# Two transformer blocks on one core: block 2's second expert product turned, small expert blocks of block 1 with both halves side by side, and block 2's bias rows made in block 1

## The chip, the cores and the metric

The kernel runs on one core of a Trainium2 chip. The core has five engines with instruction streams of their own: PE (TensorE, matmuls; PEld is its weight load, which overlaps), DVE (VectorE), ACT (ScalarE), POOL (GpSimd) and SP (SyncE), which here only issues transfers. Sixteen DMA engines move data between DRAM and the on-chip memory; SP, ACT and POOL each issue transfers on a queue of their own. Each engine works through its instructions in the order in which they are written and waits by semaphores.

The metric is the device time of one launch in microseconds (us). Before the change three runs took 2931.6, 2932.4 and 2934.65 us, median 2932.4.

## The reference

512 tokens of 1024 features go through two blocks, all in fp32, cut here to what the change touches:

```
# block 1: retention + differential attention, then a two-level top-2 MoE
x = x + g1 * (merged @ w_out)
h2 = rmsnorm(x, norm_ffn) * (1 + sc2) + sh2
gp = softmax(h2 @ w_rg + b_rg); g_top, g = top_k(gp, 1)          # 4 groups
e_val, e = top_k((h2 @ w_re + b_re)[g], 2)                       # of 8 experts
for each chosen expert (32 in all, inner size 512):
    y = (silu(xb @ w1[e]) * (xb @ w3[e])) @ w2[e]
x = rmsnorm(x + g2 * sum(y * weight), norm_final)
# block 2: banded attention with a relative bias, pooling mixer, PEER
s = q k^T / 8 + rel_bias[t5_bucket(j - 128 - i)]                 # 8 heads, band of 192 keys
x = x + concat(attention, pool) @ w_out
h = rms_norm(x, norm2_g)
# PEER: 16384 experts of one row each, 8 heads, 16 chosen per head
act = gelu(h . u[expert]);  x = x + sum(gate * act * v[expert])
```

## The kernel before

**Numbers.** Every large fp32 product is made of three matmuls of half-width parts: a weight chunk `raw` (128 x 1024, 512 KB) is copied into a rounded part `hi` by ACT (L363) and the rest `lo = raw - hi` by DVE or now and then POOL (L365); the other operand is split in the same way. x.h, x.l and (rest of x).h add up in a PSUM bank of 128 x 512. There are eight banks, handed out and taken back by `B.get` and `B.put`.

**The stream of weights.** `Stream` (`W`) loads all chunks in the order of their use, on SP's queue (L352), each as soon as one of a few raw buffers is free, and splits them up to `W.ahead` chunks ahead.

**The order.** The instruction order of each engine is the order in which the Python code issues them. While a product runs, the code calls `tick()` after every few matmuls; each call advances the generators of `side` by one step (at most `side.most` of them live at once), or one step of the row work. So a generator's place in `side`, and the number of ticks, fix where its instructions stand between the others on every engine.

**Block 1's experts.** After the mixers, routing sorts the 1024 token-expert pairs into blocks of one expert each. The first two and the last three slots have 128 rows; slot z in between has min(128, 1024/(z+2)) rows rounded up to eights: 64 at z = 14 down to 40. Per block `gather` fetches rows on POOL, `turn` transposes and splits them, `gate_up` (L1479) makes both first products with the token rows as the stationary operand (r columns) and 512 columns of weights moving, `turn_a` transposes the result, `down` (L1537) makes the last product and `scatter` (L1522, write on POOL L1530) writes rows to DRAM. One expert of a small block takes 12 chunks and 72 matmuls of 512 columns.

**The end of block 1's mixers.** `go(MG, ev_x1, j)` is the product with w_out; per output row block a `rows_of` generator makes the squares (ACT L541), the products for norm and router (PE L526) and the transposes (PE L544) beside the running product.

**The start of block 2.** `combine` loads and adds the expert rows, `norms` makes the norm statistics (POOL and DVE L529, then DVE L536), and `band_bias` (L1765) makes the bias of the attention band: a product of bucket indicators with the bias table gives 8 rows of 511, POOL writes each 128 times to DRAM (`lb_d`, 2 MB, L1771) and loads it back with a skewed address (L1773).

**PEER.** The first 384 tokens are treated densely: `u_block` multiplies 128 experts' u rows with the tokens and takes gelu, 24 matmuls of 384 columns; `weigh` multiplies by the gates and splits; `v_group` (L2437) makes the second product for four blocks, with chunks of v as the stationary operand (128 experts x 128 features) and the 384 weighed token columns moving, 24 matmuls per block, output transposed (features x tokens). Each pair of v chunks ends in four DVE adds out of PSUM into the running sum `X4` (L529), eight adds per group. Half of the u blocks was computed in a stage before and waits in DRAM; in the last stage (the V stage, 32 groups) the groups alternate between held ones and ones whose u blocks are made just ahead. The last 128 tokens go by rows (`rows_out`, L2280): POOL gathers each expert row (L2291), DVE makes the dot and the weighted sum (L2308, L532), paced by ticks.

Of the kernel before, what the change touches and what calls it, by code (L numbers as in the profile page):

```python
# [22 lines left out]
P = 128  # L23
# [92 lines left out]
RG = 8  # L116


def block_rows(z):

    if z < NSTAT or z >= NE - NBIG:
        return P
    return min(P, -(-(2 * S // (z - NSTAT + NBIG + 1)) // RG) * RG)


def _konst():
# [28 lines left out]
    put("same32", e[:, None] == np.arange(NE)[None, :])  # L155
    dyn = e >= NSTAT
# [45 lines left out]
def _arrays(i):  # L202
# [28 lines left out]
    r["v"] = n["peer_v_2"][0].reshape(32, 2, 2, P, 2, 512).transpose(0, 4, 1, 3, 2, 5)  # L231
# [245 lines left out]
def build(tc, a, out, dump=None, stop=None):  # L477
# [171 lines left out]
    for i, g in enumerate(SEQ):  # L649
        if i + 1 < NG and SEQ[i + 1] >= AHEAD:  # L650
            add(U[4 * SEQ[i + 1]:4 * SEQ[i + 1] + 4])
        add([flat(a["v"][g, s, m]) for s in range(2) for m in range(2)])
# [81 lines left out]
    def body():  # L734
# [489 lines left out]

        xg = [get(2, True) for _ in range(3)]
# [3 lines left out]
        side.push(shift_rows())  # L1229
# [232 lines left out]

        def turn(z):
            hi, lo = [], []
            x = xg[blocks.index(z) % 3]
            r = block_rows(z)
            for s in range(2):
# [9 lines left out]
        act_t = {}  # L1477

        def gate_up(zs):  # L1479
            xs = [xts.pop(z) for z in zs]  # L1480
# [29 lines left out]
        def turn_a(z):  # L1510
            t = act_t.pop(z)
            ps = B.get()
            r = block_rows(z)
            for q in range(4):
# [7 lines left out]
        def scatter(o, z):  # L1522
            y = yo[len(sc_ins) % 3]
            r = block_rows(z)
            acp(y[:r, :512], o[0][:r], AF.Copy, scale=gtab[:r, z:z + 1])
            ts(y[:r, 512:], o[1][:r], gtab[:r, z:z + 1])
# [10 lines left out]
        def down(zs, direct=False):  # L1537
# [3 lines left out]
            for i in range(4):  # L1541
                j, wh, wl = W.get()
                for (hi, lo), ps in zip(xs, o):
# [8 lines left out]
            for x, ps, z in zip(xs, o, zs):  # L1552
                put(x)
# [8 lines left out]
        def add_back(o, z):  # L1562

            parts = []
            r = block_rows(z)
            for n in range(2):
# [48 lines left out]
        dve.tensor_copy(toke, src_i)  # L1615
        yo = []

        def gate_places():
# [29 lines left out]
            mm(tab[:, 256:256 + NSLOT], tabT, perm, True, True)  # L1648
            yield
# [106 lines left out]
        onb, relb, lrow, band = get(), get(), get(), get()  # L1756
        nc.scalar.dma_start(onb[:32, :511], a["buckets"])
        nc.scalar.dma_start(relb[:32, :8], a["relb"])
# [6 lines left out]
        def band_bias():  # L1765
            ps = B.get()
            mm(ps[:8, :511], relb[:32, :8], onb[:32, :511], True, True)
            pool.memset(lrow[:8, 511:512], 0.0)
            acp(lrow[:8, :511], ps[:8, :511])
            B.put(ps)  # L1770
            pool.dma_start(lb_d[:], lrow[:8, :].unsqueeze(1).to_broadcast([8, P, 512]))  # L1771
            lb = lb_d[:]
            pool.dma_start(bmv, bass.AP(tensor=lb.tensor, offset=lb.offset + 127,  # L1773
                                        ap=[[511, P], [P * 512, 8], [1, 256]]))
            yield
# [3 lines left out]
            put([onb, relb, lrow, band])  # L1779
# [629 lines left out]
        X4 = [get(3, tight=True).ap for _ in range(2)]  # L2409
# [27 lines left out]
        def v_group(ws, last):  # L2437
            for s in range(2):
                bs = [B.get() for _ in range(4)]
                for m in range(2):  # L2440
                    c = W.get()
                    for d in range(4):
                        ps = bs[d][:, :ND]
                        for b in range(2):
                            o = b * 512 + d * P
                            h, l = c[1][:, o:o + P], c[2][:, o:o + P]
                            xh, xl = (x[:, :ND] for x in ws[2 * m + b])
                            mm(ps, h, xh, m + b == 0, False)
                            mm(ps, h, xl, False, False)
                            mm(ps, l, xh, False, m + b == 2)  # L2450
                        tick()
                        if m:
                            o = X4[s][:, d * ND:(d + 1) * ND]
                            tt(dve, o, o, ps, OP.add)
                            B.put(bs[d])
                            if last:
                                oc = (4 * s + d) * ND
                                (nc.sync, nc.scalar)[d % 2].dma_start(out[:, oc:oc + ND], o)
                    W.done(c[0])
            for x in ws:  # L2460
                put(x)
# [20 lines left out]
        for i in range(-1, NG):  # L2482
            if i == 0:
                for n in range(2):
                    nc.sync.dma_start(X4[n], flat(x4_d[:, 4 * n:4 * n + 4]))
# [11 lines left out]
            if w_c is not None:  # L2497
                v_group(w_c, i == NG - 1)
# [61 lines left out]

# [17 lines left out]
```

## Time and profile before

| what | value |
|---|---|
| runs | 2931.6, 2932.4, 2934.65 us, median 2932.4 |
| profiled execution | 2930.98 us, span 2929.2 us, mean granted PE clock 0.962 |
| busy share of the span | PE 93%, PEld 80%, DVE 76%, ACT 43%, POOL 26% |
| chain that ended last | PE 49%, DVE 29%, DMA 7%, issue 7%, ACT 7% |
| chain by line, first entries | PE bank L522 44%, DVE lo L365 7%, DVE arena L529 6% |
| DRAM traffic | 625.27 MB read, 62.06 MB written, 235 GB/s |

A busy share is an average over stages, so it does not tell what bounds one of them; the windows by stage do. In the views of instructions a row stands for one or several neighbouring instructions of a line: start, length, engine, line, operation, out<-in, tile sizes and count, and in square brackets the engine's idle time before it and what ended that. A matmul's length contains its way through the array, so neighbouring matmuls overlap: the distance from start to start is the time that one costs.

### The profile page before, as it was taken

How to read it: one execution, taken by the hardware profiler on the slowest of the kernel's cores; microseconds unless marked ns; L12 is line 12 of the kernel's file. 1: busy time of each engine (PE TensorE's matmuls, PEld its weight loads, DVE VectorE, ACT ScalarE, POOL GpSimd, SP SyncE). 2: the span in 40 equal slices, each digit the busy share in tenths (PEclk: the TensorE clock that was granted, in tenths of full speed). 3: DMA queues.
4: the chain of work that ended last, by engine and by line, in shares of the span. 5: the costliest groups of instructions: out<-in, count | busy, mean ns of one | idle time of the engine just before them, and what ended most of it. 6: DMA issues, size and time to landing. Idle time of an engine off the chain costs nothing.

```text
span 2929.2 us, 40594 instructions
## 1 busy us (share of the span) xinstructions
PE 2726.5 (93%) x14351; PEld 2342.7 (80%) x14351; DVE 2238.9 (76%) x4096; ACT 1262.3 (43%) x1859; POOL 757.6 (26%) x669
## 2 busy tenths in 40 slices
PE   6999999988999999985799988999999999999999
PEld 5887888877877665544567888899899999999999
DVE  7554566548898878863558998999688888888887
ACT  3432344345676766751334233444333333333332
POOL 6110021111212111101424555222132332333231
PEclk8999999998999999996899999999999999999999
DMA  6546322347998989975223335888989989999895
GB/s 221 165 124 208 130 73 72 119 140 248 351 323 320 341 305 334 353 247 113 68 69 113 97 118 186 294 293 295 306 296 300 306 287 311 296 297 312 283 304 187
DMA packets 242211, 673.83 MB, mean 230 GB/s; under 512 B 26497, under 2 KB 94513, under 8 KB 238288
## 3 DMA queue, kind: packets, MB, share of 16 engines
q1 hardware_dynamic: 176224, 467.14, 47.3%
q0 software_dynamic: 48256, 156.44, 15.9%
q10 hardware_dynamic: 17520, 47.57, 4.5%
q8 instruction: 115, 1.88, 0.3%
q14 instruction: 96, 0.79, 0.1%
HBM read 625.27 MB, written 62.06 MB: 235 GB/s over the span
## 4 chain that ended last, share of the span: by engine, by line
PE 49%; DVE 29%; DMA 7%; issue 7%; ACT 7%; POOL 1%; ACTq 0%; DVEq 0%; POOLq 0%; SPq 0%
PE bank L522 44%; DVE lo L365 7%; DVE arena L529 6%; DVE arena L532 4%; ACT hi L363 4%; DVE arena L2308 3%; PE bank L526 3%; PE bank L544 2%; DVE arena L538 2%; DVE arena_r L529 2%; ACT arena_r L541 2%; DMA lb_d<-arena 2%; DMA raw<-in_w_in_dram 1%; DMA raw<-in_w_ret_o_dram 1%; ACT arena L541 1%
## 5 line engine op out<-in xcount | busy, mean ns | idle before, releaser
L522 PE MATMUL bank<-arena_r,hi 128*128 128x384 f32 (+1 forms) x5792 | 1618.5, 360 | 42.0 <-DVE arena L529 29.0
L522 PEld LDWEIGHTS bank<-arena_r,hi 128*128 128x128 f32 x5792 | 1066.6, 192 | 123.2 <-issue 39.0
L522 PE MATMUL bank<-arena_r,lo 128*128 128x384 f32 (+1 forms) x2896 | 1032.1, 356 | 22.3 <-POOL lo L365 15.9
L365 DVE TENSOR_TENSOR lo<-raw,hi 128x1024 fp32r<-128x1024 f32 x490 | 602.7, 1242 | 219.9 <-ACT hi L363 215.1
L522 PEld LDWEIGHTS bank<-arena_r,lo 128*128 128x128 f32 x2896 | 554.2, 191 | 65.0 <-POOL lo L365 18.5
L363 ACT ACTIVATE hi<-raw 128x1024 fp32r<-128x1024 f32 x513 | 523.5, 1051 | 176.7 <-DMA raw<-in_v_dram 56.4
L541 ACT ACTIVATE arena<-bank 128x512 f32<-128x512 f32 (+7 forms) x478 | 251.2, 535 | 569.6 <-PE bank L522 437.7
L522 PE MATMUL bank<-hi,arena_r 128*128 128x512 f32 (+10 forms) x1064 | 346.2, 396 | 7.5 <-DVEq L2548 6.2
L541 ACT ACTIVATE arena_r<-arena 128x384 fp32r<-128x384 f32 (+1 forms) x160 | 87.5, 547 | 495.1 <-DVE arena L529 447.9
L529 POOL TENSOR_TENSOR arena<-arena 128x512 f32<-128x512 f32 (+10 forms) x172 | 180.8, 1069 | 380.3 <-ACT arena L541 274.3
L2291 POOL DMA_INDIRECT arena<-in_ur_dram,idx_i x128 | 156.0, 1219 | 401.0 <-DVE arena L2308 393.4
L2291 POOL DMA_INDIRECT arena<-in_vr_dram,idx_i x128 | 157.2, 1228 | 362.6 <-DVE arena L532 337.5
L522 PE MATMUL bank<-arena_r 128*128 128x512 f32 (+12 forms) x956 | 232.9, 398 | 4.4 <-DVE arena_r L538 4.4
L522 PEld LDWEIGHTS bank<-hi,arena_r 128*128 128x128 f32 (+10 forms) x1064 | 161.5, 152 | 89.9 <-issue 7.9
L529 DVE TENSOR_TENSOR arena<-arena,bank 128x384 f32<-128x384 f32 (+6 forms) x314 | 167.9, 570 | 72.3 <-PE bank L522 72.1
L522 PE MATMUL bank<-lo,arena_r 128*128 128x512 f32 (+10 forms) x532 | 209.2, 393 | 1.3 <-DVE lo L365 1.3
L522 PEld LDWEIGHTS bank<-arena_r 128*128 128x128 f32 (+10 forms) x956 | 151.4, 162 | 70.9 <-issue 4.3
L1530 POOL DMA_INDIRECT y_d<-arena,dst_i x34 | 53.0, 1558 | 502.1 <-ACT hi L363 212.4
L529 DVE TENSOR_TENSOR arena_r<-arena,arena_r 128x384 fp32r<-128x384 f32 (+1 forms) x160 | 94.6, 591 | 103.4 <-ACT arena_r L541 103.3
L532 DVE SCALAR_TENSOR_TENSOR arena<-arena 128x1024 f32<-128x1024 f32 (+3 forms) x136 | 165.5, 1217 | 0.2
L2308 DVE SCALAR_TENSOR_TENSOR arena<-arena 128x1024 f32<-128x1024 f32 x128 | 156.0, 1219 | 0.0
L529 DVE TENSOR_TENSOR arena<-arena 128x384 f32<-128x384 f32 (+8 forms) x272 | 125.3, 481 | 23.6 <-DMA arena<-g_d 9.9
(171 smaller groups left out, 2827.1 us busy)
## 6 DMA issues: line engine op xcount, KB each, us to landing
raw<-in_u_dram SPq DMA_DIRECT2D x128, 512.0 KB
raw<-in_v_dram SPq DMA_DIRECT2D x128, 512.0 KB
raw<-in_w_down_dram SPq DMA_DIRECT2D x72, 512.0 KB
raw<-in_w_gate_dram SPq DMA_DIRECT2D x70, 512.0 KB
raw<-in_w_up_dram SPq DMA_DIRECT2D x68, 512.0 KB
arena<-in_w_up_dram SPq DMA_DIRECT2D x60, 512.0 KB
arena<-in_w_gate_dram SPq DMA_DIRECT2D x58, 512.0 KB
raw<-in_w_in_dram SPq DMA_DIRECT2D x57, 512.0 KB
```

What stands on the lines that cost most here:

```text
L363: self.nc.scalar.activation(h, r, AF.Copy)
L365: e.tensor_tensor(l, r, h.bitcast(F32), op=OP.subtract)
L522: pe.matmul(ps, l, r, start=start, stop=stop)
L526: pe.matmul(ps, l, r, start=start, stop=stop, skip_group_check=True)
L529: e.tensor_tensor(o, x, y, op=op)
L532: dve.scalar_tensor_tensor(o, x, s, y, op0=op0, op1=op1)
L538: (e or dve).tensor_scalar(o, x, s1, s2, op0=op0, op1=op1)
L541: act.activation(o, x, f, **kw)
L544: pe.transpose(ps, x, kk("ident")[:n, :n])
L1530: i = pool.indirect_dma_start(out=y_d[:], out_offset=IOA(ap=dst_i[:r, z:z + 1], axis=0), in_=y[:r], in_offset=None, bounds_check=2 * S - 1 ...
L2291: pool.indirect_dma_start(out=b, out_offset=None, in_=a[tab], in_offset=IOA(ap=idx_i[:, j:j + 1], axis=0))
L2308: dve.scalar_tensor_tensor(b, b, 1.0, h3, op0=OP.mult, op1=OP.mult, accum_out=s_[:, j:j + 1])
```

## The change

1. **V stage.** `v_group` becomes `v_block`: the weighed tokens are the stationary operand (three tiles of 128 tokens, hi and lo parts) and the v rows move, 512 columns at a time: 18 matmuls of 512 columns per block. The sums of all 32 groups stay in six PSUM banks (`acc`) until the end, so there are no adds by DVE; two banks are left for the u blocks. The residual goes in as 24 fp32 products with the identity at the first group (`residual_in`). Its load goes on ACT's queue at the start of the stage. At the end six banks are copied out, by ACT and DVE in turn, and written in six transfers. v lies in DRAM in plain rows.
2. **Paired small blocks.** Slots 14 to 28 get exactly 64 rows. hi and lo of the rows lie side by side in 128 stationary columns (`beside`); `mm_pair` makes one matmul of all 128 columns with the weights' hi part and one of the 64 hi columns with the lo part: 48 matmuls instead of 72 per expert. The two halves of the result stand in the two halves of the partitions; for the first products they are added by eight small matmuls with `fold` in `turn_a`, for the last one in `scatter` (ACT, then DVE, for each half of the columns).
3. **Bias rows.** The product and the write to `lb_d` become a generator `bias_rows`, pushed with `shift_rows` ahead of the last product of block 1's mixers; its two small loads and the write are issued by SP. At the start of block 2 ACT issues the load of the finished band; `band_bias` keeps the last addition.

```diff
+        def bias_rows():
+            lrow, relb = get(), sm(8)
+            nc.sync.dma_start(lrow[:32, :511], a["buckets"])
+            nc.sync.dma_start(relb[:32], a["relb"])
+            for _ in range(4):
+                yield
+            ps = B.get()
+            mm(ps[:8, :511], relb[:32], lrow[:32, :511], True, True)
+            yield
+            acp(lrow[:8, :511], ps[:8, :511])
+            B.put(ps)
+            pool.memset(lrow[:8, 511:512], 0.0)
+            yield
+            nc.sync.dma_start(lb_d[:], lrow[:8, :].unsqueeze(1).to_broadcast([8, P, 512]))
+            lrow.put()
...
-        side.push(shift_rows())
+        side.push(bias_rows(), shift_rows())
...
+        def beside(o, x, n):
+            v = o.rearrange("p (q k r) -> p q k r", k=2, r=HB)
+            x = x.rearrange("p (q r) -> p q r", r=HB)
+            acp(v[:, :, 0, :], x)
+            tt(dve, v[:, :, 1, :], x, v[:, :, 0, :].bitcast(F32), OP.subtract)
+
+        def mm_pair(ps, x, wh, wl, first, last):
+            mmx(ps, x, wh, first, last)
+            mmx(ps[:HB], x[:, :HB], wl, False, last)
...
+        def gate_up_pair(z):
...
+                        mm_pair(ps, x[:, i * P:(i + 1) * P], wh[:, c], wl[:, c], i == 0, i == KT - 1)
...
+                if k:
+                    dve.tensor_copy(y.ap, ps)
+                else:
+                    acp(y.ap, ps)
...
+            if paired(z):
+                for k, y in enumerate(t):
+                    for q in range(4):
+                        o = (4 * k + q) * r
+                        mm(ps[:, o:o + r], y[:, q * P:(q + 1) * P], kk("fold"), True, True)
+                    y.put()
+                y, o = get(), getr()
+                acp(y[:, :256], ps[:, :256], AF.Silu)
+                tt(dve, y[:, :256], y[:, :256], ps[:, 256:], OP.mult)
+                B.put(ps)
+                beside(o.ap, y[:, :256], 4)
...
+            if paired(z):
+                for n in range(2):
+                    c = y[:r, 512 * n:512 * n + 512]
+                    acp(c, o[n][HB:], AF.Copy, scale=gtab[HB:, z:z + 1])
+                    stt(c, o[n][:r], gtab[:r, z:z + 1], c, OP.mult, OP.add)
...
         def band_bias():
-            ps = B.get()
-            mm(ps[:8, :511], relb[:32, :8], onb[:32, :511], True, True)
-            pool.memset(lrow[:8, 511:512], 0.0)
-            acp(lrow[:8, :511], ps[:8, :511])
-            B.put(ps)
-            pool.dma_start(lb_d[:], lrow[:8, :].unsqueeze(1).to_broadcast([8, P, 512]))
...
-            pool.dma_start(bmv, bass.AP(tensor=lb.tensor, offset=lb.offset + 127,
-                                        ap=[[511, P], [P * 512, 8], [1, 256]]))
...
-        def v_group(ws, last):
...
-                            mm(ps, h, xh, m + b == 0, False)
-                            mm(ps, h, xl, False, False)
-                            mm(ps, l, xh, False, m + b == 2)
-                        tick()
-                        if m:
-                            o = X4[s][:, d * ND:(d + 1) * ND]
-                            tt(dve, o, o, ps, OP.add)
...
+        acc = [[B.get() for _ in range(2)] for _ in range(ND // P)]
+        def residual_in():
+            for t, bs in enumerate(acc):
+                for q in range(KT):
+                    x = xl[q // 4][:, q % 4 * ND + t * P:q % 4 * ND + t * P + P]
+                    mmx(bs[q // 4][:, q % 4 * P:q % 4 * P + P], x, kk("ident"), q % 4 == 0, False)
+                tick()
+            put(xl)
+        def v_block(x, last):
+            c = W.get()
+            for t in range(ND // P):
+                xh, xl_ = (z[:, t * P:(t + 1) * P] for z in x)
+                for n in range(2):
+                    h, l = (z[:, n * 512:n * 512 + 512] for z in c[1:])
+                    ps = acc[t][n]
+                    mmx(ps, xh, h, False, False)
+                    mmx(ps, xl_, h, False, False)
+                    mmx(ps, xh, l, False, last)
```

SP's order at the end of block 1's mixers before (out<-in; `raw_65` to `raw_68` are the four raw buffers, w_out the last product of the mixers, w_gate the first expert chunks):

```order
L352 DMA raw_67<-in_w_out_dram 128x1024
L352 DMA raw_68<-in_w_out_dram 128x1024
L352 DMA raw_65<-in_w_out_dram 128x1024
L352 DMA raw_66<-in_w_gate_dram 128x1024
L352 DMA raw_67<-in_w_gate_dram 128x1024
L352 DMA raw_68<-in_w_gate_dram 128x1024
L352 DMA raw_65<-in_w_gate_dram 128x1024
```

The same place on SP with the change (the stream's load is now L363):

```order
L363 DMA raw_67<-in_w_out_dram 128x1024
L363 DMA raw_68<-in_w_out_dram 128x1024
L1239 DMA arena<-in_buckets_dram 32x511
L1240 DMA small<-in_relb_dram 32x8
L363 DMA raw_65<-in_w_out_dram 128x1024
L1250 DMA lb_d<-arena 1024x1x512
L363 DMA raw_66<-in_w_gate_dram 128x1024
L363 DMA raw_67<-in_w_gate_dram 128x1024
L363 DMA raw_68<-in_w_gate_dram 128x1024
L363 DMA raw_65<-in_w_gate_dram 128x1024
```

Two small loads stand before the last w_out chunk, and the write of the bias rows stands between it and the first gate chunk.

POOL's order at the start of block 2 before (`y_d` holds the expert rows, `small` the norm's statistics):

```order
L1530 DMA y_d<-arena,dst_i 1024x1024
L1593 DMA arena<-y_d 128x2048 x4
L529 TENSOR_TENSOR arena<-arena 128x1024 x3
L1768 MEMSET arena 8x1
L1771 DMA lb_d<-arena 1024x1x512
L1773 DMA arena<-lb_d 128x8x256
L529 TENSOR_TENSOR small<-small,kc 128x8 x6
```

The same place on POOL with the change (the adds are now L540):

```order
L1627 DMA y_d<-arena,dst_i 1024x1024
L1703 DMA arena<-y_d 128x2048 x4
L540 TENSOR_TENSOR arena<-arena 128x1024 x3
L540 TENSOR_TENSOR small<-small,kc 128x8 x6
L1949 COPY arena<-arena 128x1
```

The norm's small operations follow the adds of the expert rows directly.

DVE's order in the middle of the V stage before (L365 splits, L2308 and L532 the row work, L529 with a bank the adds out of PSUM):

```order
L365 TENSOR_TENSOR lo_76<-raw_67,hi_70 128x1024
L529 TENSOR_TENSOR arena<-arena,bank_89 128x384
L2308 SCALAR_TENSOR_TENSOR arena<-arena 128x1024
L529 TENSOR_TENSOR arena<-arena 128x16
L529 TENSOR_TENSOR arena<-arena,bank_90 128x384
L529 TENSOR_TENSOR arena<-arena,bank_88 128x384
L529 TENSOR_TENSOR arena<-arena,bank_87 128x384
L365 TENSOR_TENSOR lo_77<-raw_68,hi_71 128x1024
L532 SCALAR_TENSOR_TENSOR arena<-arena 128x1024
```

The same place on DVE with the change (L376 splits, L2412 and L543 the row work):

```order
L376 TENSOR_TENSOR lo_76<-raw_67,hi_70 128x1024
L2412 SCALAR_TENSOR_TENSOR arena<-arena 128x1024
L376 TENSOR_TENSOR lo_77<-raw_68,hi_71 128x1024
L543 SCALAR_TENSOR_TENSOR arena<-arena 128x1024
L2412 SCALAR_TENSOR_TENSOR arena<-arena 128x1024
L376 TENSOR_TENSOR lo_78<-raw_65,hi_72 128x1024
```

The adds out of the banks are gone; splits and row work alternate.

## Rows read from the trace of the kernel before

**Rows 1.** Windows: from:to, length, PE PEld DVE ACT POOL busy, clock, DMA share, GB/s.
```profile
1183.26:1236.95 53.69, 53.69 (x253) 27.30 (x254) 47.92 (x52) 40.18 (x52) 8.11 (x9) 1.00 0.95 353
...
1265.00:1330.00 65.00, 50.53 (x205) 26.86 (x204) 46.64 (x65) 29.50 (x35) 11.66 (x11) 0.86 0.83 292
...
2400.00:2640.00 240.00, 233.38 (x1331) 231.62 (x1329) 207.08 (x295) 79.78 (x113) 73.43 (x62) 0.99 0.91 299
```

**Rows 2.** The chain that ended last, start of block 2: start, us, what.
```profile
1343.33 45.93 DMA lb_d<-arena
...
1390.51 1.71 POOL small L529
...
1392.23 0.17 DVE small L529
```

**Rows 3.** Timeline of PE, start of block 2.
```profile
1393.36 3.67 PE L522 MATMUL bank<-arena,kc 128*128 128x512 f32 x4 [27.00 <-DVE arena L536]
```

**Rows 4.** The window right after that wait.
```profile
1393.36:1397.10 3.74, 3.74 (x5) 1.70 (x6) 0.73 (x4) 0.62 (x2) 0.00 (x0) 0.54 0.46 168
```

**Rows 5.** Timeline of DVE, start of block 2.
```profile
1361.40 0.17 DVE L538 TENSOR_SCALAR small<-small 128x4 f32<-128x4 f32 x1
```

**Rows 6.** DMA queues from 1348 to 1362: packets, MB, share (q0 POOL, q1 SP).
```profile
q0 software_dynamic: 174, 0.69, 47.6%
q1 hardware_dynamic: 72, 0.26, 6.8%
```

**Rows 7.** Timeline of SP, end of block 1's mixers.
```profile
562.52 27.36 SPq L352 DMA_DIRECT2D raw<-in_w_out_dram  x6
599.88 7.97 SPq L352 DMA_DIRECT2D raw<-in_w_gate_dram  x4
```

**Rows 8.** Timeline of ACT, end of block 1's mixers.
```profile
611.49 2.94 ACT L363 ACTIVATE arena_r<-raw 128x1024 fp32r<-128x1024 f32 x3
```

**Rows 9.** Timeline of PE, end of block 1's mixers.
```profile
615.81 0.61 PE L522 MATMUL bank<-arena_r,hi 128*128 128x512 f32 x2
...
616.49 0.61 PE L522 MATMUL bank<-arena_r,hi 128*128 128x512 f32 x2
...
617.17 0.95 PE L526 MATMUL bank<-kc,arena 128*128 128x1 f32 x8
```

**Rows 10.** Timeline of PE, small experts of block 1.
```profile
1192.04 5.72 PE L522 MATMUL bank<-arena_r 128*40 128x512 f32 x24
...
1260.14 0.39 PE L522 MATMUL bank<-hi,arena_r 128*40 128x512 f32 x1
1260.45 0.44 PE L544 MATMUL bank<-kc,arena 40*128 40x40 f32 x4
```

**Rows 11.** Timeline of DVE, small experts of block 1.
```profile
1193.01 4.62 DVE L365 TENSOR_TENSOR lo<-arena,hi 128x1024 fp32r<-128x1024 f32 x4
...
1200.64 0.68 DVE L529 TENSOR_TENSOR arena<-arena,bank 40x512 f32<-40x512 f32 x1 [0.74 <-PE bank L522]
```

**Rows 12.** Timeline of PE in the V stage.
```profile
2400.05 0.51 PE L522 MATMUL bank<-arena_r,hi 128*128 128x384 f32 x2
...
2400.57 0.51 PE L522 MATMUL bank<-arena_r,hi 128*128 128x384 f32 x2
```

**Rows 13.** Groups by line and shape from 2280 to 2640: count, busy us, mean ns.
```profile
L522 PE MATMUL bank<-arena_r,hi 128*128 128x384 f32 x1316 | 338.1, 338 | 11.4 <-DVE arena L529 11.3
...
L529 DVE TENSOR_TENSOR arena<-arena,bank 128x384 f32<-128x384 f32 x107 | 53.9, 547 | 0.0
```

**Rows 14.** Waits from 2280 to 2860: us in total, times, longest us.
```profile
PEld bank L522 <- issue: 27.0, 12, 3.9
PE bank L522 <- DVE arena L529: 23.5, 10, 3.6
```

**Rows 15.** Timeline of ACT, gelus of a group late in the V stage.
```profile
2868.71 0.47 ACT L541 ACTIVATE arena<-bank 128x384 f32<-128x384 f32 x1
...
2873.14 0.47 ACT L541 ACTIVATE arena<-bank 128x384 f32<-128x384 f32 x1
```

More of the change, by code (lines that the diff above doesn't have):

```diff
@@ L116 @@
 RG = 8
+HB = P // 2
 def block_rows(z):
@@ L1466, in turn @@
             r = block_rows(z)
+            if paired(z):
+                ps = B.get()
+                for q in range(KT):
+                    tr(ps[:, q * r:(q + 1) * r], x[:r, q * P:(q + 1) * P], r)
+                t = getr(2)
+                beside(t.ap, ps, KT)
+                B.put(ps)
+                xts[z] = t
+                return
             for s in range(2):
@@ L1477, in body @@
         act_t = {}
+        def gate_up_pair(z):
+            x = xts.pop(z)
+            t = []
+            for k in range(2):
+                ps = B.get()
+                for q in range(4):
+                    j, wh, wl = W.get()
+                    for s in range(2):
+                        i = 2 * q + s
+                        c = slice(512 * s, 512 * s + 512)
+                        mm_pair(ps, x[:, i * P:(i + 1) * P], wh[:, c], wl[:, c], i == 0, i == KT - 1)
+                    W.done(j)
+                    tick()
+                y = get()
+                if k:
+                    dve.tensor_copy(y.ap, ps)
+                else:
+                    acp(y.ap, ps)
+                B.put(ps)
+                t.append(y)
+            x.put()
+            act_t[z] = t
         def gate_up(zs):
+            if paired(zs[0]):
+                return gate_up_pair(zs[0])
             xs = [xts.pop(z) for z in zs]
@@ L1565, in add_back @@
             r = block_rows(z)
+            pair = z < NE and paired(z)
+            if pair:
+                r = P
             for n in range(2):
@@ new lines, in body @@
+        acc = [[B.get() for _ in range(2)] for _ in range(ND // P)]
+        def residual_in():
+            for t, bs in enumerate(acc):
+                for q in range(KT):
+                    x = xl[q // 4][:, q % 4 * ND + t * P:q % 4 * ND + t * P + P]
+                    mmx(bs[q // 4][:, q % 4 * P:q % 4 * P + P], x, kk("ident"), q % 4 == 0, False)
+                tick()
+            put(xl)
[3 more added lines that the diff above has]
+                xh, xl_ = (z[:, t * P:(t + 1) * P] for z in x)
+                for n in range(2):
+                    h, l = (z[:, n * 512:n * 512 + 512] for z in c[1:])
[3 more added lines that the diff above has]
+                    mmx(ps, xh, l, False, last)
+                    if last:
+                        y = get()
+                        if n:
+                            acp(y.ap, ps)
+                        else:
+                            dve.tensor_copy(y.ap, ps)
+                        oc = t * D + n * 512
+                        (nc.sync, nc.scalar)[n].dma_start(out[:, oc:oc + 512], y.ap)
+                    if not (n and t == 1):
+                        if (t, n) != (2, 1):
+                            tick()
+            W.done(c[0])
+            put(x)
@@ L2497, in body @@
             if w_c is not None:
-                v_group(w_c, i == NG - 1)
+                for b, x in enumerate(w_c):
+                    v_block(x, i == NG - 1 and b == 3)
     def overflow(src_i, add_back):
```

77 lines of the change are left out of this document (41 added, 36 removed).

## The prediction

> **What bounds the kernel now.** I read the windows by stage first, then the chain of waits in the one long hole, then the timelines around the three places that the change touches. In the windows the reader is to see that TensorE (PE) is close to full wherever the change works: all of 53.69 us over three small experts of block 1, and 233.38 of 240 us in the V stage, the last 850 us [rows 1]. So a matmul saved counts there only as far as VectorE (DVE) or the transfers do not take its place: DVE is busy 47.92 of the 53.69 us, and the transfers have a share of 0.95 in that window and 0.91 in the V stage [rows 1]. The chain shows the hole: the 2 MB write of bias rows to DRAM is issued at 1343.33 and takes 45.93 us, and a small POOL operation of the norm at 1390.51, which only queues behind the bias rows on POOL, ends last before PE goes on [rows 2]. PE waits 27.00 us for it [rows 3], and runs at a granted clock of 0.54, the lower of its two levels, for the 3.74 us after it [rows 4].
>
> **Part 1, the wait at the start of block 2 goes.** Without the bias write and the load on POOL's queue, the norm's POOL step follows its DVE operation of 1361.40 directly [rows 5]: 1361.57 + 1.70 on POOL, then 0.17 on DVE, and from there the 1.13 us between the chain's DVE row and PE's start (1393.36 - 1392.23): 1364.6. PE is busy with its products until 1366.4 (1393.36 - 27.00), so nothing is left of the wait. Gone: 27.00, and half of the 3.74 us at the lower clock, 1.9; less whatever the POOL step meets by then, 1. T1 = -28 (bounds -20, if the chain behind it has another late member, to -29). The load of the finished band goes on ScalarE's (ACT) queue at the start of block 2, issued earlier than now (the write that it follows is long done), so it cannot be later: 0.
>
> **Part 2, the same write moved to the end of block 1's mixers.** It is not gone: buckets, bias table and the write now stand in SP's queue, the queue of all weight loads, ahead of the first expert's gate chunks. The last mixer load is issued at 562.52 + 27.36 = 589.9, so the write can go out at about 591, once its row is made by then; the gate loads now go out from 599.88 [rows 7]. How long the write holds its transfer engines: 45.93 us in the chain; the lower bound is its packets, 0.476 x 16 x 14 us / 174 = 0.613 us each [rows 6], of which each of 8 source rows has 64: 39 us. While it ran in block 2, a 512 KB weight load issued on the other queue had moved only 0.26 MB after 14 us [rows 6]: half of it sat behind the write. The first gate chunk sits behind the same write, on the same queue. It lands, then, not soon after 600 but at 630 to 637.
>
> The Trainium skill ("DMA: Bandwidth & Descriptors", section "Queues, rings and completion order") says that on each transfer engine the descriptors of one queue's ring are consumed in ring order; the half load of [rows 6] fits that, though it was on another queue. By the rule the gate chunk cannot overtake the write; if it could, that would be the first rival below.
>
> Who waits: ACT's order puts three splits of the gate chunks (2.94 us) at 611.49, ahead of the operations that make the router's rows for the next row block [rows 8]; PE's product with these rows stands at 617.17 [rows 9], and PE's own products behind it cannot pass. So PE stops at about 617 and goes on when the chunks have landed, three splits and a square are through (3.5 us): 633.7 to 641, a stall of 17 to 24; I take 22, nearer the measured 45.93 than the packets' sum. Beside it 1.9 for the lower clock after the stall as in [rows 4], and the moved bias product, at most 3.67/4 = 0.9 [rows 3], in this stretch with PE full 0.5. T2 = +24 (bounds: +0.5, if the loads do not wait, to +30, if the write goes out later because its row is late on ACT). If the stall is hidden, what hides it would be PE work of the mixers ordered before the row products, and the order gives none.
>
> **Part 3, fifteen small experts with both halves side by side.** PE per expert: 72 matmuls of 512 columns become 48. 24 take 5.72 with the last one's tail, so 0.2317 from start to start [rows 10]: 16.7 become 11.1, with transposes and eight folds about 13.5 against 53.69/3 = 17.9 now. DVE does not shrink: four splits take 4.62 [rows 11], twelve 13.9, and the rest of its 47.92/3 = 16.0 is small operations. The change adds on it the copy of one product, the second halves of two splits and a second pass in the scatter: six operations of 256 to 512 columns for five small ones, by the 0.68 of one on 512 [rows 11] 5 x 0.68 = 3.4 in place of 2.1: 17.3. So the period goes to DVE's 17.3 plus handoffs, against 17.9: 0.3 to 0.6 less. Twelve chunks of 512 KB per expert, 6.29 MB, at 353/0.95 = 372 GB/s for a full share are 16.9 [rows 1], so transfers allow little more. Twelve of the fifteen lie where PE is full; the last three end in the window 1265 to 1330, where PE has 50.53 of 65 us, behind loads: 0 there. T3 = 12 x -0.35 = -4. Bounds: -9 (period 17.2, and 1 us at the end) to +13 (a DVE gap of 1 us per expert, since a full DVE hides no wait for ACT).
>
> **Part 4, the V stage.** Three matmuls of 384 columns take 2400.57 - 2400.05 = 0.52 [rows 12], so 0.1733 each; three of 512 columns, with the same full stationary operand, 616.49 - 615.81 = 0.68 [rows 9], 0.2267 each. V has 3072 of the first (532.4) and would have 2304 of the second (522.3): -10 in all. More lies in waits. In 360 us stand 1316 matmuls with a hi part, two of every three, so 1974 [rows 13]; two groups (four u blocks and eight V blocks) hold 288, so a period of 52.5, of which 288 x 0.1733 = 49.9 is matmul. The waits are for DVE's adds out of PSUM (23.5 us, 10 times) and issue behind them (27.0, 12 times) over 580 us [rows 14]. These adds go: 107 of 0.547 in the 360 us [rows 13], 16 per period, 7.7 to 8.8 us. DVE's busy 207.08 of 240 [rows 1], 45.3 per period, falls to 37, with the ACT handoffs in `weigh` about 42. So DVE is late no longer; next are the transfers: share 0.91 x 52.5 / 49.3 = 0.97, above the 0.95 of the experts' window. PE per period: 96 x 0.1733 + 144 x 0.2267 = 49.3; with a little lost to transfers 50.1, 2.4 less than now. Over 15.5 periods -37. Added: 24 fp32 products of 128 columns for the residual, priced by a fp32 product of 512 at the lower clock, 0.92 [rows 3], a quarter 0.23, half of that at the full clock: 2.8 to 5.5, I take 4. The load of the residual moves from SP to ACT's queue at the start of the stage, ahead of the first group of u blocks, which hides it: 0 (uncovered, 1.5 MB at the 299 GB/s of [rows 1], 5 us). At the end six evacuations replace eight adds and the last transfers are fewer and larger: 0 to +1. T4 = -33 (bounds -48, no waits left, to 0, below).
>
> **Sum.** -28 + 24 - 4 - 33 = -41 on the profiled 2930.98 us (1.8 of it outside the span of 2929.2): 2890. The median shown is 1.4 above that execution, so 2892.
>
> **The rivals.**
> 1. The gate loads do not wait behind the write (its packets run faster beside idle engines, or its row is ready much earlier). For: the transfers have under half their capacity used there, and 591 is only my reading of when the row is made. Against: [rows 6]. T2 = +1: 2869. Chance 0.20.
> 2. The V stage gives its gain back. Six of eight banks hold sums, so the u blocks have two: the next u block can start only when ACT has taken a bank, and its gelus stand 4.43 apart where they follow each other [rows 15], against 24 x 0.1733 = 4.16 of PE. A coupling of 2 us per group of u blocks, 16 groups, is 32; the transfers at 0.97 could cost as much. For: ACT's order mixes these gelus with splits that wait for loads. Against: 4.43 includes DVE waits that go. T4 = 0: 2925; chance 0.12, half of it within 2927 to 2938.
> 3. Slower. In a pair the stationary operand alternates between 128 and 64 columns with every matmul. If PE does not run on through such a switch, each matmul shows its full length, 0.39 to 0.40, in place of 0.2317 [rows 10]: 48 x 0.163 = 7.8 on 13.5, 21.3 per expert against 17.9; times 12 = +41 for T3: 2937. It decides as soon as a switch costs more than (17.9 - 13.5)/48 = 0.09. Against: the one switch in the trace, from a 512-column matmul at 1260.14 to 40-row transposes at 1260.45, lies 0.31 apart, 0.08 above the spacing [rows 10], which DVE's 17.3 would still cover. Chance 0.08.
>
> The Trainium skill ("TensorEngine Tiling (Array Packing)", section "Key Properties") says that a change of tiling mode drains TensorE, which is the third rival's mechanism if 64 columns count as another mode; the 0.31 of [rows 10] speaks against a full drain here.
>
> **Chances.** The forecast 0.60, the rivals 0.20, 0.12, 0.08. Below 2926.5 is faster by over 0.2% (about what a measurement of this kernel can tell from no change), to 2938.3 the same: faster 0.60 + 0.20 + 0.06 = 0.86, same 0.06 + 0.02, slower 0.06. The likeliest case with T2's and T4's bounds, 2872 to 2912; for 8 in 10 it reaches down into the first rival and up toward the second: 2864 to 2920.
>
> **What would show it.** T1: POOL's norm step right after 1361, no PE hole there. T2: a PE hole of 17 to 24 us right after the router rows' product near 617, with the write in the transfers and ACT's gate splits waiting for their load; without it the first rival. T3: DVE near 100% and PE under 85% in the window of the small experts, 17.2 to 17.6 each; the third rival shows 0.39 between starts with PE full. T4: no waits for DVE in the V stage, transfers near 0.97, a period near 50. The forecast is wrong if the stall or the V gain is off by more than 20 us.

## The result and the profile after

The changed kernel takes 2868.58 us (median of 4 runs, 2864.65 to 2872.04), the kernel before on the same chip 2933.53: a ratio of 0.9777, 95% interval 0.976 to 0.9795. Forecast were 2892, range 2864 to 2920. The direction and all four signs came out; the gain is 65 us where 41 were forecast, and how much of that was luck is said below.

Where it went is read from landmarks, the start of the same instruction in both profiled executions (span 2929.2 before, 2864.4 after), and the step from one landmark to the next is what a stage gained or lost:

| landmark | before | after | difference | step | forecast |
|---|---|---|---|---|---|
| last weight split by ACT before the bias rows | 560.2 | 556.4 | -3.8 | -3.8 | none |
| first store of the router's rows by ACT (mixers done) | 652.3 | 674.1 | +21.9 | +25.7 | T2 +24 |
| POOL's load of the expert rows (block 1 done) | 1314.1 | 1326.5 | +12.4 | -9.5 | T3 -4 |
| first load of gates for the V stage | 2077.6 | 2054.7 | -22.9 | -35.3 | T1 -28 |
| end | 2929.2 | 2864.4 | -64.8 | -41.9 | T4 -33 |

The first step lies ahead of every changed instruction. In a kernel that changes nothing before block 2 (the turned second product alone, below) this landmark lies at 556.8, so it is no part of the change.

**The stall in the mixers is there.** SP's timeline after: the bias write goes out at 586.79, one gate load behind it.

```profile
585.75 0.35 SPq L363 DMA_DIRECT2D raw<-in_w_out_dram  x1
586.79 0.85 SPq L1250 DMA_DIRECT2D lb_d<-arena  x1
595.06 7.53 SPq L363 DMA_DIRECT2D raw<-in_w_gate_dram  x1
```

ACT's and PE's timelines after: ACT's split of that load, which started at 611.49 before [rows 8], waits 23.23 us for it, and the product with the router's rows, at 617.17 before without a wait [rows 9], waits 21.64 us for ACT.

```profile
632.18 1.06 ACT L374 ACTIVATE arena_r<-raw 128x1024 fp32r<-128x1024 f32 x1 [23.23 <-DMA raw<-in_w_gate_dram]
...
636.32 1.87 PE L537 MATMUL bank<-kc,arena 128*128 128x1 f32 x8 [21.64 <-ACT arena L552]
```

**The wait at block 2's start is gone, and the slow stretch ahead of it is shorter.** POOL's timeline after: the norm's step follows 25.25 us behind the adds, with nothing between.

```profile
1341.58 2.35 POOL L540 TENSOR_TENSOR arena<-arena 128x1024 f32<-128x1024 f32 x1 [0.22 <-DMA arena<-y_d]
1369.18 2.61 POOL L540 TENSOR_TENSOR small<-small,kc 128x8 f32<-128x8 f32 x1 [25.25 <-DVE small L549]
```

The windows from the first product of block 2 to where the clock rises, before and after (length, PE and the other engines busy, granted clock, share, GB/s), show what the prediction did not count: in both PE is busy throughout, at the lower clock level in most of it, but before for 21.5 us and after for 7.7.

```profile
1335.90:1357.40 21.50, 21.45 (x74) 16.59 (x74) 7.75 (x10) 11.76 (x19) 1.14 (x1) 0.54 0.49 84
```

```profile
1350.90:1358.60 7.70, 7.64 (x28) 5.64 (x28) 6.53 (x9) 7.70 (x14) 0.00 (x0) 0.60 0.72 193
```

**The experts.** Two windows after: the first holds the one large two-block step among the small experts with its neighbours, the second six small experts in a row; then the same stretches before.

```profile
1074.50:1130.40 55.90, 55.90 (x281) 44.66 (x280) 48.67 (x53) 39.71 (x52) 15.27 (x10) 1.00 0.87 317
1136.60:1244.50 107.90, 95.70 (x446) 64.93 (x446) 101.87 (x109) 86.49 (x110) 11.97 (x18) 0.92 0.94 352
```

```profile
1052.30:1118.00 65.70, 65.70 (x313) 46.43 (x312) 47.77 (x52) 38.44 (x51) 8.54 (x8) 1.00 0.78 283
...
1123.70:1231.00 107.30, 107.30 (x505) 56.04 (x504) 96.22 (x104) 80.62 (x103) 16.28 (x18) 1.00 0.96 352
```

Six small experts take 107.9 us where they took 107.3: nothing is won there, PE has 12 us of idle time instead, and DVE is busy for 101.87. The window with the large step is 9.8 us shorter, about the whole of T3's step: there PE was the bound before (65.70 of 65.70, DVE 47.77) and still is.

Alternating the stationary operand costs no drain. PE's timeline after: 128 and 64 columns follow each other every 0.23 us, as the equal ones did [rows 10].

```profile
1104.10 0.39 PE L537 MATMUL bank<-hi,arena_r 128*128 128x512 f32 x1
1104.33 0.39 PE L537 MATMUL bank<-lo,arena_r 128*64 128x512 f32 x1
1104.56 0.40 PE L537 MATMUL bank<-hi,arena_r 128*128 128x512 f32 x1
```

**The V stage.** The window after that answers to the last of [rows 1]: PE is busy for all of it, and the list of PE's waits from 2250 to 2830 is empty, where it had the two of [rows 14].

```profile
2400.00:2640.00 240.00, 240.00 (x1172) 212.82 (x1171) 188.91 (x240) 88.49 (x121) 89.90 (x66) 1.00 0.93 318
```

1172 matmuls at 240 per two groups are 4.88 periods of 49.1 us. Without a count of matmuls, by the starts of DVE's splits in `weigh` (eight per two groups), fourteen periods take 690.8 us (2109.6 to 2800.4), 49.3 each, which is PE's own time by the prediction's prices; before they took 740.6 (2127.3 to 2867.9), 52.9 each. Forecast were 50.1 and 52.5.

### The profile page after: what moved, and what is told of

Read it like the earlier page. It is cut to its first block, busy times and chain, and to the rows that moved or that the text cites. A ratio compares the mean times of both kernels' runs of the same rounds, so it can differ in the third digit from the quotient of the medians.

```text
span 2864.4 us, 38446 instructions
## 1 busy us (share of the span) xinstructions
PE 2655.4 (93%) x13453; PEld 2239.4 (78%) x13453; DVE 2138.9 (75%) x3858; ACT 1285.0 (45%) x1876; POOL 796.8 (28%) x667
## 4 chain that ended last, share of the span: by engine, by line
PE 34%; DVE 15%; issue 2%; DMA 2%; ACT 1%; POOL 1%; ACTq 0%; another core or an unknown queue 0%; POOLq 0%; DVEq 0%
PE bank L537 19%; PE bank L533 15%; DVE arena L549 3%; DVE lo L376 2%; DVE arena L540 2%; DVE arena_r L540 1%; DVE arena L543 1%; DVE arena L2236 1%; DVE arena L2243 1%; DVE arena L2238 1%; DVE arena L2412 1%; DVE arena L2302 1%; ACT arena L552 1%; DMA arena<-g_d 1%; POOL arena L540 1%
## 5 line engine op out<-in xcount | busy, mean ns | idle before, releaser
L533 PE MATMUL bank<-arena_r,hi 128*128 128x384 f32 (+1 forms) x3744 | 1084.0, 370 | 16.7 <-ACT arena L552 7.5
L376 DVE TENSOR_TENSOR lo<-raw,hi 128x1024 fp32r<-128x1024 f32 x490 | 602.5, 1244 | 223.4 <-ACT hi L374 213.2
L533 PEld LDWEIGHTS bank<-arena_r,hi 128*128 128x128 f32 x3744 | 687.8, 191 | 92.9 <-issue 8.2
L533 PE MATMUL bank<-arena_r,lo 128*128 128x384 f32 (+1 forms) x1872 | 683.8, 365 | 21.1 <-POOL lo L376 16.6
L537 PE MATMUL bank<-hi,arena_r 128*128 128x512 f32 (+1 forms) x2224 | 667.4, 375 | 33.9 <-ACT arena_r L552 13.0
L552 ACT ACTIVATE arena<-bank 128x512 f32<-128x512 f32 (+5 forms) x496 | 259.6, 533 | 648.7 <-PE bank L533 499.0
L537 PEld LDWEIGHTS bank<-hi,arena_r 128*128 128x128 f32 x2224 | 411.2, 192 | 122.5 <-ACT hi L374 24.0
L537 PE MATMUL bank<-lo,arena_r 128*128 128x512 f32 (+2 forms) x1232 | 467.4, 379 | 12.0 <-DVE lo L376 12.0
L533 PEld LDWEIGHTS bank<-arena_r,lo 128*128 128x128 f32 x1872 | 356.2, 190 | 63.4 <-POOL lo L376 19.1
L540 POOL TENSOR_TENSOR arena<-arena 128x512 f32<-128x512 f32 (+10 forms) x172 | 181.2, 1071 | 380.1 <-ACT arena L552 271.6
L537 PEld LDWEIGHTS bank<-lo,arena_r 128*128 128x128 f32 (+1 forms) x1232 | 223.9, 182 | 63.2 <-DVE lo L376 23.0
L533 PE MATMUL bank<-hi,arena_r 128*128 128x512 f32 (+6 forms) x584 | 189.3, 395 | 0.0
L540 DVE TENSOR_TENSOR arena_r<-arena,arena_r 128x384 fp32r<-128x384 f32 (+2 forms) x175 | 100.8, 576 | 110.2 <-ACT arena_r L552 110.0
L543 DVE SCALAR_TENSOR_TENSOR arena<-arena 128x1024 f32<-128x1024 f32 (+3 forms) x136 | 166.3, 1224 | 12.6 <-DMA arena<-in_vr_dram,idx_i 12.3
L2412 DVE SCALAR_TENSOR_TENSOR arena<-arena 128x1024 f32<-128x1024 f32 x128 | 156.9, 1225 | 11.1 <-DMA arena<-in_ur_dram,idx_i 10.9
L540 DVE TENSOR_TENSOR arena<-arena 128x384 f32<-128x384 f32 (+8 forms) x272 | 126.0, 484 | 45.6 <-ACT arena L552 30.3
```

The source lines that it names most:

```text
L376: e.tensor_tensor(l, r, h.bitcast(F32), op=OP.subtract)
L533: pe.matmul(ps, l, r, start=start, stop=stop)
L537: pe.matmul(ps, l, r, start=start, stop=stop, skip_group_check=True)
L540: e.tensor_tensor(o, x, y, op=op)
L543: dve.scalar_tensor_tensor(o, x, s, y, op0=op0, op1=op1)
L552: act.activation(o, x, f, **kw)
```

## The experiments

Times are compared with the kernel before on the same chip (2931.4 to 2933.7 us).

**Each part alone.** Three kernels, each the kernel before with one part of the change.

> The kernel before with the bias rows' part alone. Theory: two terms of opposite sign, read from where the two traces stand apart: -36 us at the start of block 2 (the 27.0 us wait, and PE's lower clock before and after it) and +26 us at the end of block 1's mixers (ACT's gate split waits some 23 us for its load behind the bias write, PE 21.6 us for ACT): -10, about 2923 us, with a PE hole of 19 to 24 us near 615. Rival: the 7 us at block 2's start beyond the wait and its clock have nothing to do with this part (another alignment of the clock after the experts): then -29 + 26 = -3, about 2930 us.

2927.88 us, ratio 0.9981 (0.997 to 0.9992). Both terms are there. PE's wait in the mixers:

```profile
642.07 1.87 PE L526 MATMUL bank<-kc,arena 128*128 128x1 f32 x8 [22.72 <-ACT arena L541]
```

Against the kernel before, ACT's splits are 27 us later after the mixers and 32 us earlier again after block 2's start. The 32 lie between theory (36) and rival (29); the measured -4.8 does too.

> The kernel before with the paired small expert blocks alone. Theory: DVE bounds the paired experts, so six experts in a row still take 17.9 to 18.0 us each with PE at about 89% there, and the gain is the 9 to 10 us around the one large two-block step between them, where PE was late and now is not: -10, about 2923 us. Rival A: the period falls as the prediction had it, 17.3 to 17.6 each, -4 to -9, spread evenly. Rival B: the 10 us came from the stall ahead of the experts (loads that had run ahead), then 0: 2933 us.

2923.68 us, 0.9965 (0.9954 to 0.9975): -9.0, the theory. Six small experts take 107.9 us here too, and the step falls at the large one. Rivals A and B fall. This kernel still makes the bias rows in block 2, and there its PE is again at the lower clock for 27.5 us:

```profile
1329.80:1357.30 27.50, 27.45 (x96) 21.99 (x96) 7.75 (x10) 11.77 (x20) 1.15 (x1) 0.53 0.48 80
```

But the length of that stretch does not go with the bias work. The turned second product alone (next) also makes the rows there and leaves the lower clock after 9.9 us (first window below). The band part alone, which does not, leaves it after 3.7 us but falls back 3.4 us later for another 9.6, and the kernel further down that writes on ACT's queue and keeps the buffer, which does not either, falls back to it for most of 17.9 us (second window):

```profile
1335.80:1345.70 9.90, 9.86 (x31) 6.14 (x31) 6.53 (x9) 9.90 (x18) 1.14 (x1) 0.57 0.40 103
```

```profile
1341.10:1359.00 17.90, 17.86 (x70) 16.13 (x70) 2.00 (x2) 5.52 (x9) 0.00 (x0) 0.53 0.19 60
```

Nor does the stretch cost anything where POOL's step behind the bias work decides: the norm's product on PE starts at 1393.36 before [rows 3], and with the turned second product alone at the same time, after a wait that is longer by what PE was earlier:

```profile
1393.34 3.78 PE L522 MATMUL bank<-arena,kc 128*128 128x512 f32 x4 [32.46 <-DVE arena L536]
```

From the first product of block 2 to this one PE takes 57.4 us before, 30.4 of work and 27.0 of wait. The changed kernel takes 22.8, and the eight other kernels that make the rows in block 1, with the same instructions here, 22.8 to 30.7, by where the clock falls and rises. So (21.5 - 7.7)/2 = 7, what T1 was short of, came with the clock; nothing shows that this part of the change brings it.

> The kernel before with the turned second product alone. Theory: the V stage becomes bound by PE alone, 49.3 us per two groups instead of 52.5, no PE waits from 2250 on: -42 us, about 2891 us. Rival: transfers or the two free banks take part of it back when the stage is reached at another time: -33 us or less, about 2900 us.

2886.94 us, 0.9839 (0.9821 to 0.9857): -45.7, somewhat over the theory. The three parts alone sum to -59.5 against -65 together; the runs of one kernel spread by 3 to 12 us, so whether the rest is an interaction stays open, the more so as the clock at block 2's start alone differs by up to 8 us from kernel to kernel.

**Does the write have to be slow?**

```diff
-            lrow, relb = get(), sm(8)
+            lrow, relb, rep = get(), sm(8), get()
...
+            dve.tensor_copy(rep[:32, :P].rearrange("p (h g) -> p h g", g=16),
+                            relb[:32].unsqueeze(2).to_broadcast([32, 8, 16]))
-            mm(ps[:8, :511], relb[:32], lrow[:32, :511], True, True)
+            mm(ps[:, :511], rep[:32, :P], lrow[:32, :511], True, True)
...
-            nc.sync.dma_start(lb_d[:], lrow[:8, :].unsqueeze(1).to_broadcast([8, P, 512]))
+            nc.sync.dma_start(lb_d[:].rearrange("h (g j) c -> (h g) j c", j=8),
+                              lrow.ap.unsqueeze(1).to_broadcast([P, 8, 512]))
```

> The changed kernel with the bias rows made 16 times over (the bias table repeated in 128 stationary columns, one matmul as before), so that the 2 MB write leaves from 128 partitions and not from 8. Theory: the write was slow because 8 source rows feed 8 of the 16 transfer engines with packets of 0.61 us; from 128 rows it takes under 12 us, ACT's gate split waits under 3 us, and the kernel takes 22 us less than the changed one: about 2846 us. Rival: the packets are slow because of their target or their kind (a broadcast write of 2 to 4 KB into DRAM), and stay slow: 1024 packets on 16 engines at 0.6 us are again 39 us, and nothing is won: 2869 us.

2842.37 us, 0.9696 (0.9675 to 0.9717): 26 us less than the changed kernel, the theory. The DMA view of 586 to 595 us holds the whole write:

```profile
DMA packets 1184, 2.62 MB, mean 291 GB/s; under 512 B 32, under 2 KB 32, under 8 KB 1184
...
q1 hardware_dynamic: 1184, 2.62, 81.5%
```

2 MB and the last mixer chunk in under 9 us, where 8 source rows took some 45. Neither ACT nor PE waits for a gate chunk any more; the splits after the mixers lie 2 us later than in the kernel before, set against those ahead of the bias rows.

**Is it SP's queue or the engines?**

```diff
-            nc.sync.dma_start(lb_d[:], lrow[:8, :].unsqueeze(1).to_broadcast([8, P, 512]))
+            nc.scalar.dma_start(lb_d[:], lrow[:8, :].unsqueeze(1).to_broadcast([8, P, 512]))
```

> The changed kernel with the slow bias write (8 source rows) issued by ACT in place of SP, all else as changed. Theory: the order within SP's queue made the stall; on another queue the two streams take turns on each engine, so a gate chunk's eight packets per engine wait for eight of the write's (0.61 us each), some 6 us, and PE's wait near 617 falls from 21.6 to 0 to 8 us: 2847 to 2856 us. Rival: the eight engines themselves are held, on whatever queue, as the half load in block 2 looked; then the gate chunk lands only when the write is through and the time stays near 2869 us.

2861.87 us, 0.9749 (0.9732 to 0.9765), between the two; the profiled execution, 2870.92, is the longest of four. Its waits from 600 to 640 us (total, times, longest) show a second one that no theory had:

```profile
ACT arena L552 <- DMA lb_d<-arena: 10.2, 1, 10.2
...
PEld bank L555 <- ACT arena L552: 9.2, 1, 9.2
PE bank L555 <- ACT arena L552: 9.1, 1, 9.1
ACT arena_r L374 <- DMA raw<-in_w_gate_dram: 9.0, 3, 4.8
...
PE bank L537 <- ACT arena L552: 7.0, 1, 7.0
```

The gate chunks now land before the write is through, so PE waits only 7.0 for them; then ACT wants the buffer that the write still reads. A kernel that gives this buffer back only after the mixers (`held_row.append(lrow)` in place of `lrow.put()`):

> As the slow write on ACT's queue, but the bias rows' buffer is given back only when the mixers are through, so that no later operation has to wait for the write to have read it. Theory (that run's 22 us were two waits one after the other: about 12 us for the gate chunks that share engines with the write, and 10.2 us of ACT for the buffer): the second goes, about 10 us less than the changed kernel's 2869: 2850 to 2860 us, ACT's wait for lb_d is gone from the list of waits, the waits for the gate chunks stay at some 9 us. Rival (whatever ends first, PE waits for the write itself, since the loads behind it stay slow until it is through): the stall stays 20 us and more, 2862 to 2870 us.

2857.92 us, 0.9734 (0.9719 to 0.9749): the theory. The two totals are too near each other for their spread, so the stage decides: from the last split ahead of the bias rows to the router's first store, the landmarks of T2, this kernel takes 12.1 us more than the kernel before the change, the write on ACT's queue alone 22.0, the changed kernel 25.7 and the spread write 1.3. PE's one wait is left, with the gate chunks':

```profile
ACT arena_r L374 <- DMA raw<-in_w_gate_dram: 9.4, 3, 5.1
...
PE bank L537 <- ACT arena L552: 7.5, 1, 7.5
```

So the stall had two layers. PE's wait went from 21.6 to 7.5 us and the stage from +25.7 to +12.1: half to two thirds is the order within one queue, most of the rest is shared engines. On its own queue the write still slows the gate chunks, by the DMA view of 595 to 625 us (KB each, median us from issue to landing) by more than the 6 us of turns that I had put down; a w_out chunk ahead of the write landed after 3.4 us in the changed kernel:

```profile
raw<-in_w_gate_dram SPq DMA_DIRECT2D x4, 512.0 KB, 19.7
```

**What paced the V stage before?**

```diff
+        junk = get()
+        pool.memset(junk.ap, 0.0)
...
             W.done(c[0])
             put(x)
+            for _ in range(2):
+                tt(dve, junk[:, :ND], junk[:, :ND], junk[:, :ND], OP.mult)
```

> The changed kernel with two products of 128x384 by DVE per v block, on a buffer of their own, that nothing waits for: as many DVE operations as the adds that went, without their tie to PSUM banks. Their result is not used. Theory (DVE's load set the pace before): 16 x 0.55 = 8.8 us more on DVE per two groups, 38.8 + 8.8 and 5 of handoffs = 52.6 against PE's 49.3; PE waits again for the weighed tokens, +30 to +50 us, 2899 to 2919 us. Rival (the banks' release by the adds set the pace): PE stays at 100% in the stage, 0 to +6 us, at most 2875 us.

2925.46 us, 0.9975 (0.9962 to 0.9988): +57 against the changed kernel, all of the V stage's gain and 7 us above the theory's range; a period is 53.9 us by the splits in `weigh`, not 52.6. The same window with this load:

```profile
2400.00:2640.00 240.00, 226.46 (x1071) 199.99 (x1070) 207.78 (x292) 76.61 (x108) 71.15 (x60) 0.97 0.91 299
```

PE waits again (from 2284 to 2715 28.2 us for ACT, whose copies wait for DVE), with no add tied to a bank. DVE's load alone is enough for the pace before; the banks' release is not needed for it. DVE is at its end at 207.78 of 240, the same as before (207.08, [rows 1]): the rest are handoffs to ACT and back in `weigh`.

**What paces the small experts?** On the spread write, the copy of the first product goes to ACT (`acp(y.ap, ps)` for both halves):

> The spread write, and the one 128x512 copy of the paired first product moved from DVE to ACT. Theory: DVE bounds the paired experts; 0.69 us less on DVE per expert takes the period from 18.0 to 17.3, over some twelve experts -8: about 2834 us against 2842 of the spread write alone. Rival: the transfers (share 0.94) or ACT's order bound it; then the period stays 17.8 to 18.0: 2840 to 2846 us.

2837.99 us, 0.9665 (0.9648 to 0.9682), 4 us less where 8 were forecast. That is within the spread of the two kernels' runs, but six small experts decide (spread write first, then this):

```profile
1113.40:1221.30 107.90, 93.08 (x442) 63.05 (x441) 101.87 (x109) 86.82 (x109) 12.00 (x18) 0.94 0.95 352
```

```profile
1111.70:1216.00 104.30, 90.26 (x446) 61.36 (x446) 98.27 (x103) 89.26 (x115) 11.96 (x18) 0.98 0.97 364
```

-3.6 us for six copies of 0.69 less on DVE, 0.60 each: DVE paced them.

Every twelfth split on POOL besides (`W.turns = 12 if paired(x) else 0` ahead of `gate_up`):

> As the copy on ACT, and every twelfth weight split of the paired experts on POOL in place of DVE (2.5 us there, 1.15 on DVE). If DVE still bounds, another -1.1 us per expert until the transfers' 16.9 or POOL's queue decides: 2820 to 2830 us. Rival: the split queues on POOL behind the row writes, which wait for DVE, and PE waits for it: no gain or a loss, 2834 to 2860 us.

2854.85 us, 0.9731 (0.9715 to 0.9748): the rival's time, but not its reason. A small expert takes 18.4, and over six of them PE waits for ACT and DVE, never for POOL. What grew is DVE's own work, 103.40 us for six experts against 98.27 with one split more each. In every one, DVE's split that runs beside POOL's takes 3.1 us where the others take 1.22, and ends 1.1 us after POOL's:

```profile
1153.30 2.93 POOL L376 TENSOR_TENSOR lo<-raw,hi 128x1024 fp32r<-128x1024 f32 x1 [5.50 <-ACT hi L374]
```

```profile
1154.19 3.11 DVE L376 TENSOR_TENSOR lo<-raw,hi 128x1024 fp32r<-128x1024 f32 x1 [0.21 <-ACT hi L374]
```

One split off DVE saves 1.2 and the longer one costs 1.9.

One of the two sums of the scatter off DVE instead:

```diff
+                st = get()
...
-                    stt(c, o[n][:r], gtab[:r, z:z + 1], c, OP.mult, OP.add)
+                    if n:
+                        acp(st[:r], o[n][:r], AF.Copy, scale=gtab[:r, z:z + 1])
+                        tt(pool, c, c, st[:r], OP.add)
+                    else:
+                        stt(c, o[n][:r], gtab[:r, z:z + 1], c, OP.mult, OP.add)
```

> The spread write, the copy on ACT, and of the two sums in a paired expert's scatter one made by ACT and POOL (a scaled copy, an add of 64x512) in place of DVE's 0.70. If DVE's operations set the period, it falls from 17.4 to 16.9 us, where the transfers (6.29 MB at some 372 GB/s) are due next: about 2832 to 2836 us. Rival (transfers, share 0.97, or ACT, 89 of 104 us, are already the bound): the period stays at 17.3 to 17.6, 2836 to 2842 us.

2829.56 us, 0.9644 (0.963 to 0.9657), the fastest, 1.4% below the changed kernel. Six small experts:

```profile
1112.30:1212.70 100.40, 92.17 (x442) 63.08 (x442) 94.32 (x97) 92.75 (x122) 25.99 (x24) 0.94 1.00 378
```

16.7 each, and now the transfers are full: 1.00 at 378 GB/s. POOL's add (1.54 us) runs beside two DVE operations that read PSUM, and these keep the lengths that they had without it (0.73 and 0.40).

## Why the prediction was right or wrong

- **T1**, -28, measured -35: the mechanism holds (POOL's step behind the adds, no PE hole). Mis-sized is PE's work ahead of the wait: the sum left its 30.4 us as they stood and counted half of 3.74 us at the lower clock behind it; the work took 22.8. That was luck: over the nine kernels that make the bias rows in block 1, the step from the expert rows' load to the V stage is 27.5 to 35.2 us shorter than before, and the changed kernel is the one at the far end. What makes the clock rise earlier or later there stays open.
- **T2**, +24, measured +25.7: right in place, cause and size (21.6 of 22 for the wait). The first rival falls, as the half load of [rows 6] had spoken for. The ring order that the Trainium skill states ("DMA: Bandwidth & Descriptors", section "Queues, rings and completion order") agrees: on one queue the gate chunk landed only behind the write, on another queue ahead of its end.
- **T3**, -4, measured -9.5, with the step wrong: "so the period goes to DVE's 17.3 plus handoffs" left the handoffs (DVE waiting for ACT's half of a split) without a price. DVE's timeline after shows two per expert, 17.0 + 1.0 = 18.0, no gain at all; PE is at 0.89 there, where under 0.85 was the sign named, with 16.0 us per expert at a granted clock of 0.92 where 13.5 were put down:

```profile
1166.53 0.42 DVE L540 TENSOR_TENSOR arena_r<-arena,arena_r 128x256 fp32r<-128x256 f32 x1 [0.48 <-ACT arena_r L552]
1167.48 2.36 DVE L376 TENSOR_TENSOR arena_r<-raw,arena_r 128x1024 fp32r<-128x1024 f32 x2 [0.52 <-ACT arena_r L374]
```

  The gain came at the large step, which the prediction counted nowhere: there PE was the bound, and the paired experts beside it free it. The sign of T3 came out by luck.
- **T4**, -33, measured -41.9: the mechanism holds, the saving per period was 3.6 us and not 2.4. The 0.8 us "lost to transfers" is the term that failed; their share went to 0.93, not 0.97, and PE waited for nothing. The period before was 52.9, not 52.5. Fourteen periods save 50 us; the two ends of the stage give back 8, where the sum had 4 for the residual. The second rival falls: two banks are enough. That DVE's load was enough to set the pace is now shown and was only argued before.
- **The third rival** falls: 0.23 from start to start. A full drain would have cost 7.8 us per expert; none is seen. The Trainium skill ("TensorEngine Tiling (Array Packing)", section "Key Properties") has a drain at a change of tiling mode; in this trace a mere change from 128 to 64 columns shows none.
- The range held the time near its low end because three of four terms erred to the same side, for three unlike reasons: the clock's luck, a gain at a place that was not counted, and a loss to transfers that did not come.

## What to carry to other kernels

A transfer moved out of one wait is a transfer on some other queue: price it where it lands, by the queue that it joins, the engines that it holds and the buffer that it keeps, three waits that appeared here one behind the other. A saving on the bounding engine can end where the next is due, so price the next one with its handoffs, and look for steps between the regular ones that have another bound. The cure for the slow transfer here was to give it more source partitions. Work moved to an idle engine can still lengthen what the bounding engine does beside it, so read the lengths of its operations afterwards.

## What the runs showed of the hardware

A write from 8 partitions, each row 128 times, took 45 us for 2 MB; the same bytes from 128 partitions under 9. PE can be busy for 21.45 of 21.5 us and stay at a granted clock of 0.54. In kernels with the same products there such stretches lasted from 3.7 to 27.5 us, with the bias work beside them (9.9 to 27.5) and without it (3.7 to 17.9); why is open. A DVE split of 128x1024 beside a POOL split took 3.1 us in place of 1.22, while DVE operations that read PSUM kept their length beside POOL's 64x512 add.
